# A second bias buffer, a finer spread of modulation parts and a new order of mixer steps in a two-layer diffusion backbone

## The chip, the cores and the metric

The kernel runs on one core of one Trainium2 chip. The metric is the device time of one execution in microseconds (us), taken as the median of the runs shown. TensorE does the matmuls (PE in the tables, its weight loads PEld), VectorE is DVE, ScalarE is ACT, GpSimd is POOL, and SyncE (SP) computes nothing: it issues the large loads. Each engine works through its own instructions in a fixed order and waits where an input is not there yet.

## The reference

One inference step through two layers, on 128 context tokens and 256 latent tokens of width 1024, in fp32. Of each layer:

```python
def trunk_layer(x, mods, mixer_w, g_norm_l, w_gu_l, w_down_l, ctx):
    sh1, sc1, ga1, sh2, sc2, ga2 = mods
    h = modulate(rms_norm(x, g_norm_l[0]), sh1, sc1)
    mix, new_ctx = token_mixers(h, *mixer_w, ctx)
    x = x + ga1 * rms_norm(mix, g_norm_l[1])
    f = swiglu(modulate(rms_norm(x, g_norm_l[2]), sh2, sc2), w_gu_l, w_down_l)
    x = x + ga2 * rms_norm(f, g_norm_l[3])
    return x, new_ctx
```

`token_mixers` projects `h` by one combined matrix and runs three head groups on it: neighbourhood attention with a learned relative bias (4 heads), grouped-query attention with normalised and rotated q and k (8 heads), and a bidirectional mLSTM scan (4 heads). The three outputs, concatenated, go through one output projection. `swiglu` has 2816 hidden columns. The six modulation vectors of a layer come from `silu(c) @ w_ada + b_ada`, once for the context and once for the latent tokens.

## The kernel before, in words

Every fp32 weight tile is split into a rounded part `hi` (ACT, line 117) and a remainder `lo` (DVE, line 118), and each product is three fp32r matmuls, `hi*hi`, `hi*lo`, `lo*hi` (`mm3`, lines 107 to 109). Weights arrive through SP in 512 KB pieces, in a ring of three `raw` tiles (`raw_of`, line 125). A piece can be issued when the split of the piece three before it is done.

A layer has two halves. **The mixers** (function `mixers`): projections, mLSTM, attention and output projection are cut into small steps, and the string `SCHEDULE[l]` lists these steps in the order in which they are recorded. PE, DVE and ACT execute in exactly that order (`ENGINES`, `manual_schedule`); the orders of SP and POOL are laid by the tile framework. The letters that matter here:

- `f` is the next piece of a projection (`fps` and `tps` tiles) or of the output projection (`ops`); of a projection by features one `f` is 6 matmuls of 384 columns. These pieces depend on little and fill PE.
- `t` is one tick of the modulation work (`Ada.tick`): load 1 MB of `w_ada` into one of two `araw` tiles, multiply the one before it on PE (`mul_p`, line 223, tile `adap` in the one PSUM bank of tag `sm`), add the result on DVE (`acc`, lines 229 and 231).
- `L0` to `L3` load row data for four mLSTM units into a `W` tile (POOL, line 867, then a select on POOL, line 870), `E` takes exponentials on ACT (line 887), `C` makes scores on PE (line 909, tile `S`) and multiplies them with `W` on DVE (lines 896, 897, 911), `U` sums on PE (lines 922 and 926, tile `nd`) and writes `hml` through DVE. `cin` transposes the incoming states on PE (line 948, tile `ctp`); `hsum`, `hrstd`, `hnorm` normalise `hml`, and the last reader of `hml` is line 1003 on DVE.
- `bias` loads the bias windows of the neighbourhood attention, one tile `nb` for each pair of heads (`load_bias`, four SP loads per tile at line 1090, each of 64 x 6 runs of 64 floats). `K0` and `K1` transpose the cached keys (line 687) and add the column mask to the bias (line 1094, DVE).
- `c`, `e`, `p`, `v` are scores, softmax, transposes and value products of an attention unit: `sc` (line 1021, PE), `nm` (line 1027, DVE), `P` (line 1035, ACT), `ptp` (line 1050), `av` (line 1063).
- `A1` to `A4` split weight pieces ahead, until so many pairs are ready.
- `r`, `g`, `x`, `q`, `y` finish a 128-token tile (norm, gate, residual, norm), and `00` to `11` transpose it (line 354), modulate it (`xm`, line 359, ACT) and split it into `hT` (lines 363 and 364, DVE) for the second half.

**The feed-forward half** (function `ffn`): 11 steps `b2`, each with the gate and up products of 256 hidden columns (`gups`, 384 tokens) and, two blocks late, the down products (`facc`). Here the modulation vectors are multiplied on DVE (`mul_v`, line 179) and summed on PE (line 188). Its first products (`gu`) need the `hT` of tiles 0 and 1, first the half of columns 0 to 511 and then the other.

The two bias tiles before: tile 0 is a buffer of pool `mp` with the tag "R", which holds the mLSTM's gate rows until `cols` has transposed them. Tile 1 is a buffer of pool `mn` with the tag "n3", which holds `hml`.

Of the kernel before, what the change touches and what calls it, by code (L numbers as in the profile page):

```python
# [8 lines left out]
F32 = mybir.dt.float32  # L9
# [8 lines left out]
DEPTH = 2  # L18
# [2 lines left out]
NEG = -1e30  # L21
SCHEDULE = (
    (
# [8 lines left out]
    ),  # L32
    (
# [8 lines left out]
    ),  # L42
)
ENGINES = {mybir.EngineType.PE, mybir.EngineType.DVE, mybir.EngineType.Activation}
# [7 lines left out]
def hybrid_step(  # L52
# [10 lines left out]
    cp = ctx.enter_context(tc.tile_pool(name="cp", bufs=1))  # L63
# [19 lines left out]
    brow = tp.tile([96, 128], F32, tag="g2", name="brow", bufs=4)  # L83
    A.dma_start(brow, b_ada.rearrange("l (e p) -> (l e) p", p=128))
    junk = cp.tile([128, D], BF16, name="junk")
    ones = cp.tile([128, 1], F32, name="ones")
    G.memset(ones, 1.0)
    eps = cp.tile([128, 1], F32, name="eps")
    G.memset(eps, EPS)
    scol = cp.tile([128, 8, 34], F32, name="scol")  # L90
    V.memset(scol, 0.0)
# [7 lines left out]
    Amod = cp.tile([128, 2, 2, 2, 8], F32, name="Amod")  # L99
# [167 lines left out]
    def ada_start(pp):  # L267

        big = [hp.tile([128, 3, 4, 256], F32, tag=f"hT{a}", name=f"sraw{a}") for a in range(2)]
        more = ov.tile([128, 4, 4, 256], F32, tag="ov", name="sraw2")  # L270
        slots = [b[:, n] for b in big for n in range(3)] + [more[:, n] for n in range(4)]
        b1 = cp.tile([128, 8], F32, name="b1")
        V.tensor_scalar(b1, bcol[:, 0, 1], 1.0, None, ALU.add)

        def load_q(q):
            r = {}
            for h in range(2):
                for vec in range(2):
                    n = 4 * q + 2 * h + vec
                    raw = slots[n % 10]  # L280
                    e0 = vec * D + q * 256
                    SP.dma_start(raw, w_ada[0, h * 512:(h + 1) * 512, e0:e0 + 256].rearrange("(k p) f -> p k f", p=128))
                    r[vec, h] = raw
            return r

        def mod_sum(raws, hs=(0, 1), ps=None):
            ps = ps or [pp.tile([128, 512], F32, tag="b", name="sps") for _ in range(2)]
            for h in hs:
                for vec in range(2):
                    for k2 in range(2):  # L290
                        for g in range(4):
                            k = 2 * k2 + g // 2
                            fs = slice((g % 2) * 128, (g % 2) * 128 + 128)
                            PE.matmul(ps[vec][32 * g:32 * g + 32, 0:128], lhsT=scol[:, 4 * h + k, 2:34],
                                      rhs=raws[vec, h][:, k, fs], start=h == 0 and k2 == 0, stop=h == 1 and k2 == 1)
            return ps

        def mod_cols(q, ps):
            cps = pp.tile([128, 512], F32, tag="b", name="scp")
            for vec in range(2):  # L300
                rows = ap_.tile([128, 128], F32, tag="acc", name="srows", bufs=2)
                A.activation(rows, ps[vec][:, 0:128], AF.Copy)
                PE.matmul(cps[:, 4 * vec:4 * vec + 4], lhsT=rows, rhs=cst[:, C_SC:C_SC + 4],
                          start=True, stop=True)
            for n in range(2):
                f = 2 * q + n
                b, a = (cps[:, 4 * vec + 2 * n:4 * vec + 2 * n + 2] for vec in range(2))
                V.tensor_scalar(Bmod[:, 0, 0, :, f], b, bcol[:, 0, 0, f:f + 1], None, ALU.add)
                am = V.tensor_scalar(Amod[:, 0, 0, :, f], a, b1[:, f:f + 1], gcol[:, 0, 0, f:f + 1],
                                     ALU.add, ALU.mult)  # L310
            return am.ins
        return load_q, mod_sum, mod_cols
# [60 lines left out]
    def mixers(l, ma, mp, mn, pp, banks, h1T, steps, pairs, tails):  # L373
        ada = Ada(steps, pp, "sm")
# [115 lines left out]
        def tok_first(c0):  # L490
            ps = [pp.tile([128, 512], F32, tag="w", name="tps") for _ in range(3)]
            if l == 0:
                load_q, mod_sum, mod_cols = ada_start(pp)
                ws = {}

# [586 lines left out]
        nbs = {}  # L1082

        def load_bias(j):
            nbs[j] = nb = (mn if j else mp).tile([128, 2, 6, 64], F32, tag="n3" if j else "R", name="nb")
            for u in range(2):
                for hd in range(2):
                    base = na_bias[l, 2 * j + hd]
                    src = bass.AP(base.tensor, base.offset + (5 - u) * 31 - 48, [[1, 64], [31, 6], [1, 64]])
                    SP.dma_start(nb[64 * u:64 * u + 64, hd], src)  # L1090
# [6 lines left out]
        for i in (1, 2):  # L1097
            for j in range(2):
                n_units.append(Unit([(lambda j=j, i=i: N["q"][:, j, tile_slice(i)], lambda j=j: N["k"][:, j, 128:512])], 3,
                                    lambda u, b, hd, j=j: vn[:, 1 + b, j * 128 + 64 * hd:j * 128 + 64 * hd + 64],  # L1100
# [13 lines left out]
        def load_biases():  # L1114
            for j in range(2):
                load_bias(j)
# [84 lines left out]
    def ffn(l, fa, fb, pp, steps, h2T, first, tail):  # L1201
# [3 lines left out]
        ada = Ada(steps, pp, "gu", spare)  # L1205
# [83 lines left out]
        def gu(b2, raws=None, ready=(), then=None):  # L1289
            raws = raws or gu_raw(b2)  # L1290
            ready = list(ready)
            for bb in range(2):
                pss = []
                for g in range(2):
                    w = ready.pop(0) if ready else gu_w(4 * b2 + 2 * bb + g, raws[g][:, :, bb * 128:(bb + 1) * 128])
                    ps = pp.tile([128, 512], F32, tag="gu", name="gups")
                    gmm(ps, w, 0, 384)
                    pss.append(ps)
                act(2 * b2 + bb, *(ps[:, :384] for ps in pss))
                if then and not bb:  # L1300
                    then()

        def down_w(b, dst=None):
            return load_k(w_down[l], b * 128, 1, 0, 1024, dst)

        def down_mm(b, w, i, halves=(0, 1)):
            hi, lo = w[:2]
            tk = slice(i * 128, (i + 1) * 128)
            f = fT[b]
            for half in halves:  # L1310
                mm3(facc[i][half], f[0][:, tk], f[1][:, tk], hi[:, 0, HALVES[half]], lo[:, 0, HALVES[half]],
                    b == 0, b == NB - 1)
# [3 lines left out]
        for b2 in range(1, NB // 2):  # L1316
            gu(b2, *(started if b2 == 1 else ()))
            if b2 < NB // 2 - 1:
                for b in (2 * b2 - 2, 2 * b2 - 1):
                    w = down_w(b)  # L1320
                    for i in range(3):
                        down_mm(b, w, i)
                        if b2 > 1 and i:
                            with tc.issue_after(w[2]), tc.issue_after(w[3]):
                                ada.tick(2 if l + 1 < DEPTH else 1)
        ada.finish()
        last = range(NB - 4, NB)
        flat = [[t.rearrange("p k f -> p (k f)") for t in slots[n]] for n in range(2)]
# [167 lines left out]
```

## Time and profile before

| | us |
|---|---|
| runs of the kernel before | 1021.54, 1014.47, 1019.5 |
| their median | 1019.5 |
| the profiled execution | 1013.69 |
| its span, first to last instruction | 1011.9 |
| mean granted TensorE clock, as a share of full speed | 0.981 |

The profile is of one execution, which lies 5.8 us under the median of the runs. In the profile a busy time is the sum over an engine's instructions, with overlaps counted once; "idle before" is the time in which an engine stood still ahead of an instruction, with what released it. The clock of TensorE has two levels, 1.2 and 2.4 GHz; the profile gives it as a share of the higher one, so that 0.50 is a stretch wholly at the lower level.

### The profile page before, as it was taken

To read this page: it belongs to the slowest core of one execution; us is meant where nothing else is said; L and a number is where in the kernel's file an instruction comes from. 1 tells how busy PE (TensorE), PEld (TensorE's weight loads), DVE (VectorE), ACT (ScalarE), POOL (GpSimd) and SP (SyncE) were. 2 spreads that over 40 slices of the span, in tenths; PEclk is the share of its full clock that TensorE was granted. 3 is DMA by queue.
4 is the path that set the end of the run, shared out by engine and by line. 5 is a ranking of instruction groups with operands and counts; after the bars stand their busy time and mean duration, and the time that the engine had idled before them with its cause. 6 is when DMAs were issued, how large, how long until landed. Compare 5 with 4: busy or idle time off the path is not lost. (4 is left out here: it accounts for less than half of the span.)

```text
span 1011.9 us, 16033 instructions
## 1 busy us (share of the span) xinstructions
PE 960.1 (95%) x6375; PEld 847.8 (84%) x6375; DVE 620.7 (61%) x940; ACT 466.3 (46%) x920; POOL 83.4 (8%) x142
## 2 busy tenths in 40 slices
PE   5999889899999999999999989899799999999997
PEld 4789776578999999999978979666699999999996
DVE  3568547667954999959374855677577433333323
ACT  4545426678533433333375553577573333333322
POOL 0312411000001100000320230000000001000000
PEclk9999999999999999999999997999899999999999
DMA  9969768407873976945235652330756335333001
GB/s 329 306 194 244 230 206 240 124 2 250 275 234 117 322 262 226 312 167 179 73 101 152 161 153 60 91 99 2 239 183 202 125 125 167 125 125 125 21 1 63
DMA packets 128508, 167.22 MB, mean 165 GB/s; under 512 B 15664, under 2 KB 90176, under 8 KB 128432
## 3 DMA queue, kind: packets, MB, share of 16 engines
q1 hardware_dynamic: 122208, 153.93, 47.9%
q0 software_dynamic: 5856, 12.10, 4.4%
q8 instruction: 50, 0.82, 0.3%
q14 instruction: 26, 0.21, 0.1%
q10 hardware_dynamic: 368, 0.16, 0.1%
HBM read 163.46 MB, written 2.70 MB: 164 GB/s over the span
## 5 line engine op out<-in xcount | busy, mean ns | idle before, releaser
L118 DVE TENSOR_TENSOR lo<-raw,hi 128x1024 fp32r<-128x1024 f32 (+2 forms) x100 | 120.1, 1204 | 80.1 <-ACT hi L117 79.8
L117 ACT ACTIVATE hi<-raw 128x1024 fp32r<-128x1024 f32 (+2 forms) x100 | 103.8, 1041 | 97.1 <-PE facc L109 80.3
L109 PE MATMUL gups<-hT,ring 128*128 128x384 f32 x416 | 140.8, 339 | 0.0
L107 PE MATMUL gups<-hT,ring 128*128 128x384 f32 x416 | 140.7, 338 | 0.0
L108 PE MATMUL gups<-hT,ring 128*128 128x384 f32 x416 | 140.6, 338 | 0.0
L179 DVE SCALAR_TENSOR_TENSOR spare<-araw,scol,spare 128x1024 f32<-128x1024 f32 x98 | 120.7, 1279 | 0.5 <-ACT spare L177 0.4
L107 PE MATMUL facc<-hi,f 128*128 128x512 f32 x240 | 95.6, 398 | 0.0
L108 PE MATMUL facc<-lo,f 128*128 128x512 f32 x240 | 94.8, 395 | 0.0
L109 PE MATMUL facc<-hi,f 128*128 128x512 f32 x240 | 94.8, 395 | 0.0
L108 PEld LDWEIGHTS gups<-hT,ring 128*128 128x128 f32 x416 | 78.2, 188 | 0.5
L107 PEld LDWEIGHTS gups<-hT,ring 128*128 128x128 f32 x416 | 78.1, 188 | 0.5
L109 PEld LDWEIGHTS gups<-hT,ring 128*128 128x128 f32 x416 | 78.2, 188 | 0.0
L109 PE MATMUL gups<-hT,xring 128*128 128x384 f32 x224 | 75.8, 338 | 0.0
L107 PE MATMUL gups<-hT,xring 128*128 128x384 f32 x224 | 75.8, 338 | 0.0
L108 PE MATMUL gups<-hT,xring 128*128 128x384 f32 x224 | 75.7, 338 | 0.0
L107 PE MATMUL tps<-hi,hT 128*128 128x512 f32 (+2 forms) x192 | 67.4, 351 | 2.2 <-DVE hT L511 2.2
L109 PE MATMUL tps<-hi,hT 128*128 128x512 f32 (+2 forms) x192 | 65.5, 341 | 0.0
L108 PE MATMUL tps<-lo,hT 128*128 128x512 f32 (+2 forms) x192 | 65.4, 340 | 0.0
L1228 ACT ACTIVATE ring<-rgu 128x1024 fp32r<-128x1024 f32 x26 | 27.6, 1062 | 68.2 <-PE gups L108 37.8
L1228 ACT ACTIVATE ring<-spare 128x1024 fp32r<-128x1024 f32 x26 | 27.6, 1060 | 62.3 <-PE gups L108 37.4
L107 PEld LDWEIGHTS facc<-hi,f 128*128 128x128 f32 x240 | 45.2, 188 | 10.8 <-issue 1.4
L109 PEld LDWEIGHTS facc<-hi,f 128*128 128x128 f32 x240 | 45.2, 188 | 10.5
(299 smaller groups left out, 1983.0 us busy)
## 6 DMA issues: line engine op xcount, KB each, us to landing
araw<-in_w_ada_dram SPq DMA_DIRECT2D x80, 512.0 KB, 4.9
raw<-in_w_down_dram SPq DMA_DIRECT2D x44, 512.0 KB, 4.2
spare<-in_w_gu_dram SPq DMA_DIRECT2D x20, 1024.0 KB, 5.4
rgu<-in_w_gu_dram SPq DMA_DIRECT2D x20, 1024.0 KB, 5.2
raw<-in_w_in_dram SPq DMA_DIRECT2D x36, 512.0 KB, 4.8
sraw<-in_w_ada_dram SPq DMA_DIRECT2D x16, 512.0 KB, 9.5
raw<-in_w_out_dram SPq DMA_DIRECT2D x8, 512.0 KB, 5.8
G<-row POOLq DMA_DIRECT2D x8, 512.0 KB, 7.2
```

The costliest lines, as they stand in the source:

```text
L107: PE.matmul(out, lhsT=wh, rhs=xh, start=start, stop=False)
L108: PE.matmul(out, lhsT=wh, rhs=xl, start=False, stop=False)
L109: PE.matmul(out, lhsT=wl, rhs=xh, start=False, stop=stop)
L117: a = A.activation(hi[:, :n], raw, AF.Copy)
L118: v = V.tensor_tensor(lo[:, :n], raw, hi[:, :n].bitcast(F32), ALU.subtract)
L179: V.scalar_tensor_tensor(acc[s], raw[:, part], scol[:, k, 2 + s:3 + s], acc[s], ALU.mult, ALU.add)
L1228: A.activation(hi, rv, AF.Copy)
```

## The change

Four edits. (1) Both bias tiles come from pool `mp`, tile 1 under a tag of its own, "nb", so it no longer shares a buffer with `hml`. (2) To make room, `ones` and `eps` become two columns of one tile, and the eight-column helper `b1` lies in a part of `Amod` that layer 1 writes later. (3) In the feed-forward half the ticks are dealt out differently: per weight block 1, 1, 2 after the three token tiles in place of 0, 2, 2 (layer 0), and 0, 0, 1 in place of 0, 1, 1 (layer 1). (4) Both strings of `SCHEDULE` are new: the same steps, each as often as before, in another order. The instructions of each engine are the same in number and kind; their order differs. Line numbers after the change are higher by one.

```diff
 SCHEDULE = (
     (
...
-        "L3 s s C1 s s U0 E2 C2 s s U1 s f t E3 t C3 U2 f f U3 s f s s f s s t s f f hsum kT s hrstd f s hnorm f "
-        "f bias t s f A1 A2 f K1 f A2 A2 f t rT K0 f rmix s f f A2 t c0 f e0 kout c1 A2 p0 t f f e1 v0 c2 p1 t "
...
+        "L3 s s s U0 E2 C2 s ogate U1 s f t E3 U2 C3 f s f s f f U3 f t s t f s hsum hrstd kT s hnorm f s f f t "
+        "bias f A2 s s A2 f A1 K1 A2 f K0 f rT t rmix f s f f s t c0 f A2 e0 A2 kout c1 p0 t f A1 f e1 v0 c2 A2 "
...
     (
...
-        "f s f Q1 s f f Q2 f f f krow f cols decay kw f cin E0 L1 f cout C0 L2 s ogate L3 s E1 f C1 s s E2 U0 s "
-        "s s s f C2 s E3 U1 s s s s U2 s f s C3 s s s f s kT f f U3 f f f s s f bias s hsum hrstd hnorm f f f f "
...
+        "f s Q0 f Q1 f Q2 f f f krow f cols decay kw L1 E0 cin f s f cout C0 E1 L2 s L3 f s C1 s ogate s s E2 s "
+        "s U0 s C2 f E3 U1 U2 s s s s s f s s C3 s f f s f kT f f s U3 hsum s s s hrstd hnorm bias f f f f f f f "
...
-    ones = cp.tile([128, 1], F32, name="ones")
+    ones_eps = cp.tile([128, 2], F32, name="ones_eps")
+    ones, eps = ones_eps[:, 0:1], ones_eps[:, 1:2]
     G.memset(ones, 1.0)
-    eps = cp.tile([128, 1], F32, name="eps")
...
-        b1 = cp.tile([128, 8], F32, name="b1")
+        b1 = Amod[:, 1, 0, 0]
...
-            nbs[j] = nb = (mn if j else mp).tile([128, 2, 6, 64], F32, tag="n3" if j else "R", name="nb")
+            nbs[j] = nb = mp.tile([128, 2, 6, 64], F32, tag="nb" if j else "R", name="nb")
...
-                        if b2 > 1 and i:
+                        if b2 > 1:
                             with tc.issue_after(w[2]), tc.issue_after(w[3]):
-                                ada.tick(2 if l + 1 < DEPTH else 1)
+                                ada.tick(1 + i // 2 if l + 1 < DEPTH else i // 2)
```

How the instructions stand, before and after, at three places.

SP in layer 0, around the bias loads, before the change (`nb_1607` is bias tile 0, `nb_1612` tile 1; `araw` are modulation weights):

```order
L125 DMA raw_1100<-in_w_in_dram 128x8x128
L168 DMA araw_1261<-in_w_ada_dram 128x2x512
L1090 DMA nb_1607<-in_na_bias_dram 64x6x64 x2
L125 DMA raw_1175<-in_w_in_dram 128x8x128
L125 DMA raw_1467<-in_w_out_dram 128x2x512
L168 DMA araw_1617<-in_w_ada_dram 128x2x512 x2
L125 DMA raw_1598<-in_w_out_dram 128x2x512
L1090 DMA nb_1612<-in_na_bias_dram 64x6x64 x4
L168 DMA araw_1669<-in_w_ada_dram 128x2x512 x2
L125 DMA raw_1771<-in_w_out_dram 128x2x512
```

And the same place after it (`nb_1631` is tile 1, `nb_1626` tile 0):

```order
L1091 DMA nb_1631<-in_na_bias_dram 64x6x64 x2
L126 DMA raw_770<-in_w_in_dram 128x8x128
L126 DMA raw_895<-in_w_in_dram 128x4x256
L169 DMA araw_1265<-in_w_ada_dram 128x2x512 x2
L1091 DMA nb_1626<-in_na_bias_dram 64x6x64 x3
L126 DMA raw_1173<-in_w_in_dram 128x8x128
L126 DMA raw_1446<-in_w_out_dram 128x2x512
L126 DMA raw_1596<-in_w_out_dram 128x2x512
L169 DMA araw_1605<-in_w_ada_dram 128x2x512 x2
L126 DMA raw_1769<-in_w_out_dram 128x2x512
```

Tile 1, which stood between the third and the fourth output weight, now stands ahead of the last nine pieces of the input weights; tile 0 keeps its place.

SP in layer 1, before (`nb_6096` is tile 0, `nb_6101` tile 1):

```order
L125 DMA raw_5787<-in_w_in_dram 128x8x128
L1090 DMA nb_6096<-in_na_bias_dram 64x6x64 x4
L125 DMA raw_6008<-in_w_out_dram 128x2x512
L125 DMA raw_6068<-in_w_out_dram 128x2x512
L125 DMA raw_6118<-in_w_out_dram 128x2x512
L1090 DMA nb_6101<-in_na_bias_dram 64x6x64 x4
L125 DMA raw_6203<-in_w_out_dram 128x2x512
```

And after (`nb_6094` is tile 1, `nb_6089` tile 0):

```order
L126 DMA raw_5072<-in_w_in_dram 128x3x256
L1091 DMA nb_6094<-in_na_bias_dram 64x6x64 x4
L126 DMA raw_5075<-in_w_in_dram 128x3x256
L126 DMA raw_5785<-in_w_in_dram 128x8x128
L1091 DMA nb_6089<-in_na_bias_dram 64x6x64 x4
L126 DMA raw_6006<-in_w_out_dram 128x2x512
L126 DMA raw_6116<-in_w_out_dram 128x2x512
```

Tile 1 moves to the first pieces of the layer's input weights, sixteen pieces ahead of where tile 0 stands.

ACT at the end of layer 0's mixers, before (`junk` are sums of squares, `ss` their roots, `hi` a weight split, `xm` the modulation that makes the second `hT` half of tile 1, the last `x8` those of tile 2):

```order
L117 ACTIVATE hi<-raw 128x1024
L327 ACTIVATE junk,ss<-oP 128x512 x2
L331 ACTIVATE ss<-ss 128x1
L332 ACTIVATE ss<-ss 128x1
L359 ACTIVATE xm<-trp,Bmod,Amod 128x128 x4
L327 ACTIVATE junk,ss<-x 128x512
L117 ACTIVATE hi<-raw 128x1024
L327 ACTIVATE junk,ss<-x 128x512
L359 ACTIVATE xm<-trp,Bmod,Amod 128x128 x8
```

And after:

```order
L328 ACTIVATE junk,ss<-oP 128x512 x2
L332 ACTIVATE ss<-ss 128x1
L333 ACTIVATE ss<-ss 128x1
L118 ACTIVATE hi<-raw 128x1024
L328 ACTIVATE junk,ss<-x 128x512
L118 ACTIVATE hi<-raw 128x1024
L360 ACTIVATE xm<-trp,Bmod,Amod 128x128 x4
L328 ACTIVATE junk,ss<-x 128x512
L360 ACTIVATE xm<-trp,Bmod,Amod 128x128 x8
```

Two splits and one sum of squares now stand between the root and the four `xm`.

## Rows read from the trace of the kernel before

**Rows 1.** The profile page: busy time of each engine.

```profile
PE 960.1 (95%) x6375; PEld 847.8 (84%) x6375; DVE 620.7 (61%) x940; ACT 466.3 (46%) x920; POOL 83.4 (8%) x142
```

**Rows 2.** Windows by stage: length, busy us (instructions), clock, DMA share, GB/s.

```profile
75.00:153.00 78.00, 68.44 (x704) 62.95 (x706) 46.91 (x100) 34.51 (x79) 22.57 (x34) 0.98 0.76 221
153.00:240.00 87.00, 81.58 (x734) 58.68 (x735) 62.17 (x121) 62.14 (x167) 3.48 (x5) 0.98 0.48 134
240.00:515.00 275.00, 274.68 (x1608) 253.84 (x1607) 207.15 (x222) 107.98 (x147) 19.78 (x35) 1.00 0.65 218
515.00:640.00 125.00, 118.63 (x749) 107.73 (x748) 77.53 (x148) 69.23 (x154) 20.71 (x31) 0.95 0.45 119
640.00:735.00 95.00, 82.71 (x621) 60.57 (x620) 64.63 (x122) 62.08 (x171) 0.76 (x1) 0.95 0.36 113
```

**Rows 3.** PE timeline: start us, us, instruction, [idle before <- releaser].

```profile
106.44 1.08 PE L223 MATMUL adap<-araw,scol 128*32 128x128 f32 x32 [1.09 <-DVE acc L231]
...
124.61 0.63 PE L926 MATMUL nd<-share,W 128*128 128x65 f32 x4 [2.35 <-DVE hml L937]
...
148.19 0.47 PE L687 MATMUL tT<-cst,kcn 128*128 128x128 f32 x1 [4.79 <-DVE acc L231]
...
182.14 1.56 PE L1021 MATMUL sc<-kTn,qTn 64*64 64x384 f32 x8 [3.56 <-ACT P L1035]
...
604.01 1.52 PE L909 MATMUL S<-qTm,kTm 64*64 64x128 f32 x32 [3.56 <-DVE W L896]
...
612.57 1.08 PE L926 MATMUL nd<-share,W 128*128 128x65 f32 x4 [1.90 <-ACT s L138]
...
624.57 0.42 PE L107 MATMUL fps<-hT,hi 128*128 128x384 f32 x1
...
626.56 0.33 PE L109 MATMUL fps<-hT,lo 128*128 128x384 f32 x1
...
644.89 1.10 PE L1021 MATMUL sc<-share 64*64 64x128 f32 x32 [3.98 <-ACT P L1035]
...
723.09 0.55 PE L107 MATMUL gu<-hT,hi 128*128 128x256 f32 x1 [5.38 <-DVE hT L363]
```

**Rows 4.** DVE timeline, layer 0 and layer 1.

```profile
135.03 0.96 DVE L1003 TENSOR_TENSOR share<-share,hml 128x768 f32<-128x768 f32 x1
...
144.61 0.56 DVE L1094 TENSOR_TENSOR nb<-nb,cst 128x384 f32<-128x384 f32 x1 [6.64 <-DMA nb<-in_na_bias_dram]
...
239.64 0.69 DVE L364 TENSOR_TENSOR hT<-xm,hT 128x512 fp32r<-128x512 f32 x1
...
642.62 0.68 DVE L1027 TENSOR_REDUCE nm<-sc 128x4 f32<-128x512 f32 x1
```

**Rows 5.** SP timeline, layer 0.

```profile
136.01 2.62 SPq L1090 DMA_DIRECT2D nb<-in_na_bias_dram  x4
```

**Rows 6.** Windows over four short stretches, columns as in rows 2.

```profile
148.00:153.00 5.00, 4.81 (x23) 4.56 (x27) 2.33 (x5) 0.98 (x2) 3.31 (x6) 0.70 0.69 260
...
155.00:180.00 25.00, 22.60 (x256) 15.57 (x254) 17.86 (x28) 14.78 (x45) 3.48 (x5) 1.00 1.01 266
...
605.00:610.00 5.00, 4.38 (x31) 4.01 (x23) 2.88 (x9) 2.51 (x10) 2.78 (x4) 0.50 0.60 134
...
645.00:650.00 5.00, 4.96 (x45) 3.97 (x46) 3.42 (x6) 2.80 (x14) 0.76 (x1) 0.66 0.81 224
```

**Rows 7.** ACT timeline, layer 0 and layer 1.

```profile
179.74 1.06 ACT L117 ACTIVATE hi<-raw 128x1024 fp32r<-128x1024 f32 x1 [4.34 <-DMA raw<-in_w_out_dram]
...
233.01 1.10 ACT L117 ACTIVATE hi<-raw 128x1024 fp32r<-128x1024 f32 x1
...
638.50 2.00 ACT L117 ACTIVATE wT<-raw 128x1024 fp32r<-128x1024 f32 x2
```

**Rows 8.** DMA issues: count, KB each, median us from issue to landing.

```profile
raw<-in_w_in_dram SPq DMA_DIRECT2D x36, 512.0 KB, 4.8
...
nb<-in_na_bias_dram SPq DMA_DIRECT2D x16, 96.0 KB, 5.8
```

25 rows, old and new, of the table SCHEDULE are left out of this document.

## The prediction

> **What bounds the kernel.** I read the busy times first, then a table of windows by stage, then the idle time in front of PE's instructions, and last the other engines' timelines at those places. PE is busy 960.1 of 1011.9 us [rows 1], so an order alone can win only what PE waits, some 52 us, and what it loses where a wait is followed by the lower clock. The stages [rows 2] show where that lies. In the feed-forward stretch 240 to 515 PE is busy 274.68 of 275 us: nothing can be won there. The mixers have it: 78 - 68.44 = 9.6 us idle in 75 to 153, 5.4 in 153 to 240, 6.4 in 515 to 640 and 12.3 in 640 to 735. All four have a clock under 1.00. The edits touch these stages, and [rows 3] names the single waits.
>
> Where PE is busy throughout, a stretch with mean clock c costs (1 - c) times its length, since that share of the time is at half speed for twice as long. I use this below for what a wait costs after it has ended.
>
> **The bias wait of layer 0: +6.3 us.** PE stands 4.79 us before a key transpose at 148.19, for `acc` on DVE [rows 3]. DVE had itself stood 6.64 us before the mask of a bias tile, for that tile's load [rows 4]. SP had issued the load at 136.01 [rows 5], just when line 1003, which began at 135.03 and took 0.96 us, had read `hml` for the last time [rows 4]: the shared buffer is the cause. With a tile of its own the load stands ahead of nine weight pieces, long before, and tile 0's loads keep their place. So the 4.79 us go. After the wait the clock of 148 to 153 is 0.70 [rows 6], with PE nearly always busy: 0.30 x 5 = 1.5 us more. Late next would be the cached keys, whose load PE's own transposes release; the projection pieces between these and the first use stay the same, so I expect no new wait. Bounds: 0, if another input is as late, to 6.3.
>
> **The bias wait of layer 1: +4.0 us.** PE stands 3.98 us at 644.89 for `P`, which needs `nm`, which DVE began at 642.62 [rows 3, 4] behind the same kind of mask. Without the bias, `P` is limited by the two splits on ACT that end at 638.50 + 2.00 = 640.50 [rows 7]. From the end of `nm` (642.62 + 0.68 = 643.30) to the PE start were 1.59 us, so PE could start at about 642.1, 2.8 us earlier. Some 1.1 us of wait is left. The window 645 to 650 has clock 0.66 [rows 6], a loss of 1.7; after so short a wait I expect it mostly back and take 1.2. Bounds 0 to 3.98 + 1.7 = 5.7.
>
> **The mLSTM of layer 0: +1.3 us.** The last sum waits 2.35 us at 124.61 [rows 3]. Two things help now: four `f` steps stand before it where two stood, and POOL reaches the fourth `W` load two small transfers earlier. Twelve projection matmuls start from 624.57 to 626.56 [rows 3], so two `f` are 1.99 x 12/11 = 2.2 us; the wait should vanish. Against that, two ticks later on now stand back to back. The pair that did so before made PE wait 1.09 us for the single bank of `adap` at 106.44 [rows 3]. Sum 2.35 - 1.09. Bounds -1.1 to 2.4.
>
> **The mLSTM of layer 1: +3.0 us.** PE waits 3.56 us for `S` at 604.01 and 1.90 at 612.57 [rows 3], and the clock of 605 to 610 is 0.50 [rows 6]. The chain starts at the state transposes, which release the second `W` buffer. One `f` step pair (12 matmuls of 256 columns; by the price above 2.2 x 256/384 = 1.4 us) moves from ahead of these transposes to behind the scores at 604. So the chain starts 1.4 us earlier, the wait at 604 stays about 3.56, and the piece fills time before 612.57: 1.4 us won. A shorter second wait should end the low clock sooner; of the 0.5 x 4.38 = 2.2 us that this window shows, and what follows it, I take 1.6. Against it: POOL now issues the third `W` load only behind the second one's select and a store. Bounds: -2 (that delay decides) to 3.56 + 1.90 + 2.2 = 7.7; I take a value near the 1.4 and the clock, which have rows.
>
> **The end of layer 0's mixers: -1.7 us.** `hT` of tile 1's second half was done at 239.64 + 0.69 = 240.33 [rows 4], and PE went into it without a wait, having nothing else. On ACT two splits now stand between the root and `xm`; one of them stood in ACT's time ahead of the sums before (233.01 [rows 7]), and a sum of squares comes along. One split is about 1.1 us there, the sum about 0.6: the half is later by 1.7, and PE has no cover. Bounds -2.7 (both splits) to 0.
>
> **No change.** The wait of 3.56 us at 182.14 [rows 3]: ACT stood 4.34 us for an output weight [rows 7], and SP still issues the same modulation loads ahead of it; bounds -4 to +4. The 5.38 us at 723.09 [rows 3]: the chain of splits, sums and modulation before it stands as it did. The finer ticks: PE has no idle time there to win [rows 2], and in layer 1 one tick for each weight block still suffices for four loads and eight products; -1 to +1. The merged constants and `b1`: start only, 0.
>
> **Sum.** 6.3 + 4.0 + 1.3 + 3.0 - 1.7 = 12.9 us. From the profiled execution, 1013.7 us, that gives 1000.8; it was 5.8 us under the median, and from the median 1019.5 it gives 1006.6. I state 1006.5.
>
> **Rivals.** *The loads take it back.* Once layer 0 runs 7.6 us ahead (6.3 + 1.3), the attention stage asks for its weights that much sooner, and 155 to 180 already has a DMA share of 1.01 [rows 6]. Then the wait at 182.14 grows by these 7.6 us, and 5.3 remain: 1014. For it: the share. Against it: the stretch before has 0.76 [rows 2], so loads could start sooner, as far as the two `araw` and three `raw` tiles allow.
>
> *The bias loads starve the projections (slower).* Tile 1 of layer 0 now goes into the queue ahead of nine weight pieces in a stretch that feeds them. One bias DMA of 96 KB lands in 5.8 us, one of 512 KB in 4.8 [rows 8]. A feature piece feeds 24 matmuls, 4.3 us by the price above; three `raw` tiles give a lead of two, 8.6 us. If each of five pieces behind the bias slipped by a landing, 29 us, less the lead, 20 us would fall on PE: 12.9 - 20 = -7, or 1027. It decides once the slip is over 8.6 us. Against it: four bias DMAs are together less than one piece in bytes, and the quad of tile 0 stands among the last input weights in both orders.
>
> The Trainium skill speaks for this rival: "DMA: Bandwidth & Descriptors", section Specifications, asks for at least 512 B in a run for line rate and says that below it the engine reads, modifies and writes. The runs here are 256 B. If that doubled the DMA time of the quad's 384 KB, it would be another 384 KB at the 221 GB/s of the first mixer stage, 1.8 us, and the sum by it, if PE felt all of it, 11.1. The rows agree with a dear small load (96 KB slower than 512 KB), but not that PE feels it.
>
> *The bias still comes late.* If the new tile lies on memory that the half before still uses, or SP reaches it late, both bias terms fall: 12.9 - 10.3 = 2.6, or 1017. The order of SP speaks against it.
>
> **How the numbers follow.** Forecast 0.60; loads take it back 0.26; starved projections 0.07; bias still late 0.07. The range is 996 to 1019: at the low end the forecast with the clock and both mLSTM terms near their upper bounds (a gain of 23), at the high end past the second and the fourth case. About 1% of 1019.5, 10.2 us, is what a measurement can tell from no change. The forecast by its bounds lies beyond that nine times in ten, 0.54, with a little of the second case 0.56; slower by over 1% is the larger half of the starved case, 0.04; within 1% the rest, 0.40.
>
> **What would show it.** Right: no DVE wait before line 1095 (the old 1094); no PE wait before the key transposes of layer 0; a wait of about 1 us before the group scores of layer 1; none before the fourth sum of layer 0; one of about 1.7 us in the `gu` matmuls of layer 0; the 5.4 us before `gu` of layer 1 unchanged. Wrong: a wait over 7 us for an output weight in layer 0 (the first rival), waits of ACT for input weights that reach PE before 100 us (the second), or a bias load issued behind line 1004 (the third).

## The result and the profile after

| | us |
|---|---|
| kernel before, median of 19 runs (1014.47 to 1022.97) | 1018.9 |
| kernel after, median of 19 runs (1005.7 to 1014.45) | 1009.56 |
| ratio after / before, 95% interval | 0.9912 [0.9895, 0.9929] |
| first profiled execution, before / after | 1013.69 / 1013.52 |
| second profiled execution, before / after | 1017.87 / 1008.12 |

The change saves 9.0 us (0.0088 of 1018.9). I had said 12.9 us: 1006.5, in a range of 996 to 1019. The time lies in the range, 3 us above the point. The interval excludes no change; the saving of 0.9% falls just inside the "within 1%" that had 0.40, not in the "faster" that had 0.56, and the interval holds the border between the two.

The first two profiled executions hide all of this: they differ by 0.2 us, since that of before lies 5.2 us under its kernel's median and that of after 4.0 us over its own. I therefore read the change from the second pair, whose difference of 9.7 us is close to the 9.3 of the medians, and go back to more profiles below where a reading rests on it. The stages are cut at the same places of the work: first `sc` of layer 0, first `gu`, first `gups` from the extra ring, first transpose of layer 1, its first `sc`, its first `gu`, the end. Columns as in [rows 2]. The kernel before, second execution:

```profile
0.00:154.60 154.60, 132.88 (x1267) 116.21 (x1267) 83.64 (x184) 69.94 (x148) 34.71 (x64) 0.98 0.82 247
154.60:235.00 80.40, 75.14 (x660) 52.46 (x656) 56.54 (x112) 56.59 (x153) 3.48 (x5) 0.98 0.44 121
235.00:253.10 18.10, 18.10 (x130) 16.99 (x129) 13.39 (x22) 14.54 (x33) 0.00 (x0) 1.00 0.94 315
253.10:518.30 265.20, 264.89 (x1538) 244.48 (x1537) 201.42 (x215) 100.08 (x134) 19.77 (x35) 1.00 0.64 212
518.30:641.10 122.80, 114.29 (x717) 104.35 (x715) 75.83 (x144) 65.14 (x144) 20.70 (x31) 0.94 0.45 120
641.10:727.20 86.10, 73.42 (x560) 51.06 (x559) 62.08 (x119) 61.53 (x167) 0.76 (x1) 0.95 0.29 81
727.20:1016.10 288.90, 282.67 (x1518) 263.14 (x1518) 127.99 (x148) 98.30 (x145) 3.79 (x6) 0.98 0.38 123
```

And the kernel after, second execution:

```profile
0.00:149.80 149.80, 131.27 (x1263) 114.95 (x1263) 85.10 (x184) 69.71 (x148) 35.31 (x64) 0.98 0.83 255
149.80:231.30 81.50, 76.73 (x660) 53.72 (x656) 57.10 (x112) 55.75 (x152) 3.48 (x6) 0.96 0.45 120
231.30:251.70 20.40, 18.44 (x131) 17.08 (x130) 13.62 (x24) 15.52 (x34) 0.00 (x0) 1.00 0.84 281
251.70:516.90 265.20, 264.89 (x1538) 244.49 (x1537) 201.19 (x215) 100.34 (x134) 19.77 (x35) 1.00 0.65 213
516.90:636.40 119.50, 112.36 (x718) 102.62 (x717) 76.21 (x146) 65.16 (x144) 21.15 (x31) 0.96 0.47 126
636.40:716.90 80.50, 70.76 (x560) 48.99 (x559) 61.19 (x117) 61.17 (x167) 0.76 (x1) 1.00 0.26 77
716.90:1006.40 289.50, 283.24 (x1518) 263.71 (x1518) 128.68 (x148) 98.14 (x145) 3.79 (x6) 0.98 0.38 123
```

Length minus PE's busy time is what PE waited. Where the number of instructions is equal, I take a change of PE's busy time for the clock's. So every stage splits in two, the first only roughly, since its counts differ by four. Up to the first `sc` of layer 0, 4.8 us are won: 21.7 us of waits became 18.5. The attention stage of layer 0 loses 1.1 in this pair, by the clock (one low stretch of 6.8 us in place of one of 3.4). The entry of the feed-forward half loses 2.3, of which 2.0 are a new wait. The long feed-forward stage is the same to the hundredth. The mixers of layer 1 win 3.3 and then 5.6, the latter with 2.9 us fewer waits and 2.7 us less busy time for the same 560 instructions. Over the whole span, 6.0 us of the 9.7 are waits and 3.7 the clock.

PE's waits in the kernel after, second execution (columns as in [rows 3], which have those of before):

```profile
107.85 1.08 PE L224 MATMUL adap<-araw,scol 128*32 128x128 f32 x32 [0.56 <-DVE acc L232]
...
118.50 0.30 PE L242 MATMUL adat<-cst,acc 128*128 128x128 f32 x1 [1.12 <-DVE ht L941]
...
131.15 1.08 PE L224 MATMUL adap<-araw,scol 128*32 128x128 f32 x32 [0.80 <-DVE acc L232]
141.32 0.30 PE L688 MATMUL tT<-cst,kcn 128*128 128x128 f32 x1 [0.97 <-DMA kcn<-in_cache_na_kv_dram]
...
238.88 0.38 PE L108 MATMUL gu<-hT,hi 128*128 128x256 f32 x1 [1.62 <-DVE hT L364]
...
602.65 2.41 PE L910 MATMUL S<-qTm,kTm 64*64 64x128 f32 x32 [4.07 <-DVE W L897]
608.38 0.63 PE L927 MATMUL nd<-share,W 128*128 128x65 f32 x4 [0.82 <-DVE hml L938]
612.27 0.63 PE L927 MATMUL nd<-share,W 128*128 128x65 f32 x4 [1.48 <-DVE ht L941]
...
640.33 1.10 PE L1022 MATMUL sc<-share 64*64 64x128 f32 x32 [1.03 <-ACT P L1036]
...
716.93 0.55 PE L108 MATMUL gu<-hT,hi 128*128 128x256 f32 x1 [5.39 <-DVE hT L364]
```

The two waits of the bias are gone: 4.79 us in [rows 3] are now 0.97, for the cached keys and no longer for the bias, and 3.98 are 1.03. The wait of 1.62 us at `gu` of layer 0 is new, and the 5.39 at `gu` of layer 1 stand as they did. On DVE the mask of the bias, which waited 6.64 us in [rows 4], now runs without a wait:

```profile
138.85 1.96 DVE L1095 TENSOR_TENSOR nb<-nb,cst 128x384 f32<-128x384 f32 x4
```

### The profile page after: what moved, and what is told of

It reads as the page before. It is cut to its first block, busy times and chain, and to the rows that moved or that the text cites. A ratio compares the mean times of both kernels' runs of the same rounds, so it can differ in the third digit from the quotient of the medians.

```text
span 1011.7 us, 16033 instructions
## 1 busy us (share of the span) xinstructions
PE 961.7 (95%) x6375; PEld 849.1 (84%) x6375; DVE 623.4 (62%) x940; ACT 466.0 (46%) x920; POOL 83.5 (8%) x142
## 5 line engine op out<-in xcount | busy, mean ns | idle before, releaser
L118 ACT ACTIVATE hi<-raw 128x1024 fp32r<-128x1024 f32 (+2 forms) x100 | 103.8, 1042 | 100.4 <-PE facc L110 85.1
L1244 DVE TENSOR_TENSOR sg<-sg,gups 128x384 f32<-128x384 f32 x40 | 22.1, 553 | 54.1 <-PE gups L110 54.0
L108 PEld LDWEIGHTS facc<-hi,f 128*128 128x128 f32 x240 | 45.1, 188 | 10.6 <-issue 1.2
```

What stands on the lines that cost most here:

```text
L108: PE.matmul(out, lhsT=wh, rhs=xh, start=start, stop=False)
L118: a = A.activation(hi[:, :n], raw, AF.Copy)
L1244: V.tensor_tensor(sg, sg, pu, ALU.mult)
```

## The experiments

Ratios are to the kernel before, run beside each on the same chip, with 95% intervals.

### How far one profile is from its median

Both kernels unchanged, executed and profiled once more.

> The kernel before once more, for a second profile. If what a profile lies off its median by is the low clock, the low stretches of this one total more than the 40.3 us of the first profile when its time is above 1013.7 us. If not, the total is the same and the difference is in the waits.

> The kernel after once more, for a second profile. The first one, 1013.5 us, lies 4 us above its median, with a low clock at 119.5 and 6.8 us of it at 180.9. If low stretches are what the time moves by, this one, near 1009.6 us, has 5 to 8 us less of low clock than the first; if not, the total is the same.

Before: 1017.87 us. After: 1008.12 us. The low stretches in the clock record total 43.6 us (40.3 in the first profile) and 36.2 us (41.0), so both moved the way the times did, that of after by slightly less than the 5 to 8 expected. But the clock is only a part. Before, PE's busy time rose from 960.1 [rows 1] to 961.4, by 1.3 of the 4.2 us that the span grew, and the rest are waits. After, it fell from 961.7 to 957.7, 4.0 of 5.3 us. One pair of profiles can't show a change of 1%.

### The buffer alone

Both strings and the ticks are those of before; the merged constants that make room are in.

```diff
-            nbs[j] = nb = (mn if j else mp).tile([128, 2, 6, 64], F32, tag="n3" if j else "R", name="nb")
+            nbs[j] = nb = mp.tile([128, 2, 6, 64], F32, tag="nb" if j else "R", name="nb")
```

> The kernel before with the second bias buffer alone (and the merged constants that make room for it); both old orders of steps and the old ticks. My theory: the two bias waits go, 4.8 us plus clock in layer 0 and about 2.8 us plus clock in layer 1, together 10.3 us, so a ratio near 0.990 to before; in the profile no DVE wait before the mask line and no PE wait of 4.8 us before the key transposes of layer 0. Rival, the loads take it back: the wait for the output weight in layer 0 (3.56 us before) grows by most of what is won, ratio 0.995 to 0.998. Rival, the new order and not the buffer brings the gain: within 0.2% of before.

1006.61 us, ratio 0.9882 [0.9853, 0.9911]: 12 us, with an interval of 3 us on either side, so as much as the whole change saves, or more. In its profile PE has no wait of 0.3 us or more between the fourth mLSTM sum and the first `sc` of layer 0, and 1.03 us before the group scores of layer 1. The wait for the output weight in layer 0 is 4.33 us against 3.4 to 4.0 in three profiles with the shared buffer, and two later profiles with a buffer of its own and the old order of layer 0 have 2.22 and 3.31: the loads take back less than 1 us, if anything. Both rivals fall.

### The ticks alone

```diff
-                        if b2 > 1 and i:
+                        if b2 > 1:
...
-                                ada.tick(2 if l + 1 < DEPTH else 1)
+                                ada.tick(1 + i // 2 if l + 1 < DEPTH else i // 2)
```

> The kernel before with the finer spread of ticks in the feed-forward half alone. My theory: no change, -1 to +1 us, ratio 0.999 to 1.001, since PE has no idle time in that stretch. Rival: the ticks now fall on other token tiles and delay the splits of the down weights or the last modulation vectors, so that the end of the half is 1 to 3 us later, ratio 1.001 to 1.003.

1017.62 us, ratio 0.9993 [0.9966, 1.0020]. Nothing that can be measured, as expected. The interval alone would leave room for most of the 1 to 3 us of the rival, but the profile does not: its two feed-forward stages take 265.3 and 288.9 us, against 265.2 and 288.9 above.

### The old order in one layer at a time

The kernel after with one of the two strings of `SCHEDULE` taken from before, of layer 0:

> The kernel after with the old order of steps in layer 0 alone. By my terms the new order of layer 0 is worth +1.3 (fourth sum of the mLSTM) and -1.7 us (end of the mixers), so this is within 1 us of the kernel after: ratio to before near 0.990. Rival, the new order of layer 0 costs more than that: it brings a wait of about 1.6 us in the first gu matmuls, waits of 1.4 us before the modulation sums and a low clock behind them; then this kernel is 3 to 5 us faster than the kernel after, ratio to before 0.986 to 0.988. Rival, the new order of layer 0 is where the gain comes from: ratio 0.995 or more.

and of layer 1:

> The kernel after with the old order of steps in layer 1 alone. By my terms the new order of layer 1 is worth 3.0 us in the mLSTM, so this is 3 us slower than the kernel after: ratio to before near 0.994. Rival, the later load of the third row tile on the POOL queue eats it: no difference to the kernel after, ratio 0.991.

With the old layer 0: 1004.36 us, ratio 0.9863 [0.9829, 0.9897], 5 us faster than the kernel after, with an interval of some 4 us on that difference. The new order of layer 0 costs, as the first rival said. With the old layer 1: 1009.79 us, ratio 0.9915 [0.9882, 0.9947], beside 0.9912: no difference that these intervals can show.

### The new orders with the shared buffer

```diff
-            nbs[j] = nb = mp.tile([128, 2, 6, 64], F32, tag="nb" if j else "R", name="nb")
+            nbs[j] = nb = (mn if j else mp).tile([128, 2, 6, 64], F32, tag="n3" if j else "R", name="nb")
```

> The kernel after with the bias tiles sharing a buffer with hml again, as before (both new orders and the new ticks stay). My theory: the buffer is the gain, so both bias waits come back, 4.8 us before the key transposes less 2 us for the f steps that the new order puts between them and hnorm, and about 4 us in layer 1: 7 to 10 us slower than the kernel after, ratio to before 0.998 to 1.002. Rival, the new order already hides the bias load: within 2 us of the kernel after, ratio 0.991 to 0.993.

1017.82 us, ratio 0.9995 [0.9973, 1.0017]: without the buffer nothing is left of the gain. But the place isn't the one I expected in layer 0. PE's waits there, and before the group scores of layer 1:

```profile
141.84 0.30 PE L688 MATMUL tT<-cst,kcn 128*128 128x128 f32 x1 [1.25 <-DMA kcn<-in_cache_na_kv_dram]
...
173.96 0.88 PE L1064 MATMUL av<-PT,vn 128*64 128x128 f32 x12 [1.49 <-ACT PT L1054]
181.08 1.56 PE L1022 MATMUL sc<-kTn,qTn 64*64 64x384 f32 x8 [4.04 <-ACT P L1036]
...
649.24 0.99 PE L1022 MATMUL sc<-share 64*64 64x128 f32 x28 [3.43 <-ACT P L1036]
```

Before the key transposes there are 1.25 us, little more than the 0.97 with the buffer, so the new order does hide the bias load in layer 0. Longer waits stand 30 us later, 1.49 and 4.04 us. SP's timeline shows what is late there:

```profile
132.53 1.14 SPq L169 DMA_DIRECT2D araw<-in_w_ada_dram  x2
136.88 3.37 SPq L1091 DMA_DIRECT2D nb<-in_na_bias_dram  x4
140.35 6.62 SPq L169 DMA_DIRECT2D araw<-in_w_ada_dram  x4
147.08 0.41 SPq L126 DMA_DIRECT2D raw<-in_w_out_dram  x1
```

The same stretch in the kernel after:

```profile
132.29 7.61 SPq L169 DMA_DIRECT2D araw<-in_w_ada_dram  x4
140.00 0.42 SPq L126 DMA_DIRECT2D raw<-in_w_out_dram  x1
```

and of the kernel with the shared buffer, the row for this load in the view of waits of SP's queue (us in total, times, longest):

```profile
SPq L1091 <- DVE share L1004: 3.2, 1, 3.2
```

SP stands 3.2 us at the bias load until line 1004 has read `hml`, and takes another 3.4 for the four issues. The framework has also laid the output weight behind one more pair of modulation weights. It goes at 147.08 in place of 140.00, 7 us later.

These waits are not the shared buffer's alone, though. The first profile of the kernel after, where no bias load stands in this stretch, has nearly the same at this place, once for modulation weights and once for an output weight:

```profile
171.48 0.86 PE L224 MATMUL adap<-araw,scol 128*32 128x128 f32 x24 [1.33 <-DMA araw<-in_w_ada_dram]
...
182.43 1.56 PE L1022 MATMUL sc<-kTn,qTn 64*64 64x384 f32 x8 [3.87 <-ACT P L1036]
```

One profile therefore can't tell what the hold of SP costs.

### The bias load on another queue

The kernel of the last experiment, its bias still in the shared buffer, with tile 1's loads issued by POOL:

```diff
-                    SP.dma_start(nb[64 * u:64 * u + 64, hd], src)
+                    (G if j else SP).dma_start(nb[64 * u:64 * u + 64, hd], src)
```

> The kernel with the shared buffer and both new orders (ratio 0.9995), but tile 1's bias loads issued by POOL instead of SP. The load is as late as with SP, it only no longer stands in SP's queue. If the lateness of the bias itself is what the shared buffer costs: no change, ratio 0.998 to 1.001. If SP's queue, held at this load until hml has been read (136.9 us in layer 0) with weights behind it, is a good part of the cost: the waits of PE at 172 to 181 us (1.49 and 4.04 us) fall to about 2.8 us together, 2 to 3 us less, ratio 0.996 to 0.9975.

1014.43 us, ratio 0.9963 [0.9942, 0.9985]: about 3 us less, as the queue theory expected. SP's output weight is out at 139.35 again, ahead of the second pair, and PE's rows are

```profile
140.42 0.30 PE L688 MATMUL tT<-cst,kcn 128*128 128x128 f32 x1 [1.07 <-DMA kcn<-in_cache_na_kv_dram]
...
176.92 0.88 PE L1022 MATMUL sc<-kTn,qTn 64*64 64x384 f32 x8 [2.67 <-ACT P L1036]
...
644.71 1.10 PE L1022 MATMUL sc<-share 64*64 64x128 f32 x32 [4.13 <-ACT P L1036]
```

The waits of layer 0 are those of the kernel after in its second profile (0.97 us above, and 2.75 here); that of layer 1 stays.

```profile
177.45 1.56 PE L1022 MATMUL sc<-kTn,qTn 64*64 64x384 f32 x8 [2.75 <-ACT P L1036]
```

By the medians, then, the shared buffer costs the new orders some 3 us through SP's queue (0.9995 to 0.9963) and some 5 us otherwise (0.9963 to 0.9912). The 5 us lie in layer 1: from its first `sc` to its `gu` the two kernels with the shared buffer take 83.9 and 84.5 us, the kernel after 80.6 and 80.5. The 3 us are less sure. The two intervals overlap, and up to `gu` of layer 0 the two kernels take 234.7 and 229.6 us, where the two profiles of the kernel after have 235.8 and 231.3. And since SP's order changed along with the load's queue, the hold of SP and the extra pair of modulation weights are not told apart.

### Step 11 of layer 0 back ahead of the splits

One step of the kernel after moved:

```diff
-        "p13 A1 q1b b2 y1 10 A1 v13 A2 01 b2 b2 r2a r2b g2a x2a g2b x2b A1 A3 A2 A1 A1 q2a A4 11 q2b A3 A1 y2 A2 "
+        "p13 A1 q1b b2 y1 10 A1 v13 A2 01 b2 b2 r2a r2b g2a x2a g2b x2b 11 A1 A3 A2 A1 A1 q2a A4 q2b A3 A1 y2 A2 "
```

> The kernel after with one step of layer 0 moved: 11, which makes the second half of tile 1's hT, stands ahead of the weight splits again as it did before the change. My theory: the wait of 1.61 us before gu in layer 0 goes, with the low clock that follows it in some executions up to 3.4 us: ratio to the kernel after 0.9965 to 0.9985, to before 0.988 to 0.990. Rival, the splits that now come later are what the start of the feed-forward half waits for: no gain, ratio to before 0.991.

1006.3 us, ratio 0.9887 [0.9849, 0.9925], 2.5 us better than 0.9912, within the expected 0.988 to 0.990, though its interval holds 0.9912 too. The profile agrees: more than half of the new loss in the stage is gone (19.1 us from `gu` to the ring, against 20.4 in the kernel after and 18.1 before): the first `gu` products no longer wait, and a short wait for a weight split is left:

```profile
234.94 0.39 PE L110 MATMUL gu<-hT,lo 128*128 128x256 f32 x1 [0.75 <-DVE lo L119]
```

### The wait of 5.4 us in layer 1

The wait stood in both kernels, and my prediction put it down to a chain that has to be there. ACT's timeline of the kernel after shows something else:

```profile
711.65 0.64 ACT L328 ACTIVATE junk<-oP 128x512 bf16<-128x512 f32 x1
...
713.65 0.63 ACT L328 ACTIVATE junk<-oP 128x512 bf16<-128x512 f32 x1 [1.27 <-DVE ss L330]
...
714.40 0.30 ACT L332 ACTIVATE ss<-ss 128x1 f32<-128x1 f32 x1
714.73 0.20 ACT L333 ACTIVATE ss<-ss 128x1 f32<-128x1 f32 x1
714.84 1.49 ACT L360 ACTIVATE xm<-trp,Bmod,Amod 128x128 f32<-128x128 f32 x4
```

PE had made the transposes for this `xm` (step `01`, tile 1, the half that `gu` needs first) at 710.95, but ACT does them only after the sums of squares of tile 2, which wait for the last output products. The Trainium skill calls ACT, DVE and GpSimd "strict FIFO" ("Perfetto Trace Analysis", section "Tensor Engine Instruction (MATMUL, LD_WEIGHTS)"), and the trace agrees: `xm` was ready for over 3 us and stood in line. So I exchanged the two steps `01` and `11`:

```diff
-        "p11 f g1b x1b e12 x1a 00 f c13 q1a v11 p12 e13 A1 b2 v12 A1 10 p13 q1b b2 y1 v13 A2 b2 A1 A3 11 b2 r2a "
-        "g2a r2b g2b x2a x2b 01 q2a q2b y2 A4 A1"
+        "p11 f g1b x1b e12 x1a 00 f c13 q1a v11 p12 e13 A1 b2 v12 A1 10 p13 q1b b2 y1 v13 A2 b2 A1 A3 01 b2 r2a "
+        "g2a r2b g2b x2a x2b 11 q2a q2b y2 A4 A1"
```

With the old order of layer 0:

> The kernel after with the old order in layer 0 (ratio 0.986) and, in layer 1, the steps 01 and 11 exchanged: the first half of tile 1's hT, which gu needs first, is made ahead of tile 2's sums, the second half behind them. Theory: the 5.4 us before gu of layer 1 are not the chain of tile 1 but ACT's order, in which xm stands behind tile 2's two sums of squares; the wait falls to about 1 us, and with it the 6.8 us of low clock that follows: 4 to 7 us, ratio 0.980 to 0.982. Rival: the second half or tile 2 is what the end waits for, and the wait only moves some 6 us on, into gu: no gain, ratio 0.985 to 0.987.

and with the new one, `11` of layer 0 first:

> The same exchange of 01 and 11 in layer 1, with the new order of layer 0 in which 11 stands ahead of the weight splits (ratio 0.989). Theory as for the run before it: 4 to 7 us less, ratio 0.982 to 0.985; beside that run it tells whether the rest of layer 0's new order costs anything: equal within 0.2% if only the place of 11 did, 2 us slower if the modulation waits of the new order cost too. Rival: no gain, 0.988 to 0.990.

999.57 us, ratio 0.9815 [0.9788, 0.9841], and 996.98 us, ratio 0.9795 [0.9771, 0.9819], the fastest of all kernels run. Against the same kernels without the exchange (0.9863 and 0.9887) that is 4.9 and 9.4 us less, where 4 to 7 were expected, each with an interval of some 4.5 us on either side. In the profiles the two last stages together became 6.4 and 7.0 us shorter, which fits the forecast and both medians. In the profile of the second the wait and the low clock behind it are gone; its two last stages, cut as above:

```profile
631.20:707.40 76.20, 70.90 (x560) 48.98 (x560) 56.80 (x109) 58.05 (x157) 0.76 (x1) 1.00 0.23 61
707.40:994.40 287.00, 280.65 (x1518) 261.20 (x1518) 132.99 (x156) 101.38 (x155) 3.79 (x6) 0.99 0.40 130
```

```profile
707.41 0.35 PE L108 MATMUL gu<-hT,hi 128*128 128x256 f32 x1 [0.83 <-DVE hT L364]
```

The stage that ends at `gu` is 4.3 us shorter than in the kernel after (80.50), and the stage behind it takes 2.6 us less of PE for the same 1518 instructions. Nothing waits later in their place: 6.3 to 6.4 us idle in the last stage in both.

The two kernels also say what the rest of layer 0's new order is worth: 0.9815 with the old, 0.9795 with the new and `11` first; without the exchange it was 0.9863 against 0.9887, the other way round. Beyond the place of `11` these runs tell no difference between the two orders of layer 0.

### The order of layer 1 once more

> The fastest kernel so far (ratio 0.9795, 11 first in layer 0, 01 and 11 exchanged in layer 1) with the old order of layer 1, in which 01 and 11 are exchanged too. It measures the new order of layer 1 by itself once more. By my term of 3.0 us for the mLSTM of layer 1 this kernel is 3 us slower, ratio 0.982 to 0.983. Rival: the row tile's load and the exponentials behind it set the pace, and filling in behind the scores only moves the wait: the same within 1 us, ratio 0.979 to 0.981.

999.66 us, ratio 0.9824 [0.9785, 0.9862], 2.9 us above 0.9795, as my term has it, but the rival lies in the interval too. Together with the pair 0.9915 and 0.9912 (0.3 us) and the pair 0.9882 and 0.9863 (1.9 us, with the ticks in it), that is 1.7 us on average, each with an interval of some 3 to 4 us. The stage from layer 1's first transpose to its first `sc` shows no gain: with a bias buffer of its own, three profiles with the old order have 119.5 to 120.2 us and six with the new one 118.0 to 122.1, with a mean of 119.9 for both. The stage behind it, up to `gu`, is 0.7 us shorter with the new order, with and without the exchange (81.3 and 81.4 against 80.5 to 80.8; 76.8 against 76.0 and 76.2). The medians leave it open between 0 and 3 us; the profiles show 0.7.

## Why the prediction was right, and where it was not

- **Layer 0's bias wait, +6.3.** The wait went as I had said: 3.8 us in the second pair, and with it the low clock behind it (0.70 in [rows 6]; 1.00 from 141 to 146 now). With the 1.6 us less that PE is busy up to the first `sc` (four matmul records fewer), that makes 5.4. What I named as late next, the cached keys, is late now, by 0.97 us; I had priced it at nothing. And the buffer is not the only thing that does it: with the new order the wait is gone in the shared buffer too (1.25 us left), which I had not seen.
- **Layer 1's bias wait, +4.0.** Of the right size. From its first `sc` to `gu` the kernels with the old order take 85.1, 86.1 and 85.5 us with the shared buffer and 81.3 and 81.4 with one of its own: 4.2 us, with the 1.03 of wait left that I had forecast as 1.1. The 5.6 us of the second pair hold in addition the new order's 0.7 and a stretch of low clock that was 3.4 us longer in that execution of before. The two buffer terms together were 10.3; the buffer alone measured 12.0, with 10.3 inside its interval.
- **Layer 0's mLSTM, +1.3.** It is 0. The wait of 2.35 us did vanish. But I set one pair of ticks against it, and in the new order there are more waits in its place: 0.56 and 0.80 us for `acc`, 1.12 for the `ht` of the mLSTM that stands ahead of it on DVE, and two of 0.69 for a copy on ACT (line 691). Between 85 and 140 us the waits of PE over 0.2 us sum to 4.8 us before and 4.9 after, both in the second profile. The stage up to the first `sc`, which holds this term and the first, won 4.2 us in the mean (three profiles of the old order with the shared buffer, 154.5; six with both changed, 150.3), where the two terms make 7.6.
- **Layer 1's mLSTM, +3.0.** With the one before it, this is the term that I had most too large: 0.3, 1.9 and 2.9 us in three comparisons of medians, 0.7 in the profiles. The step that failed is "the wait at 604 stays about 3.56, and the piece fills time before 612.57". The chain is POOL's load of the row tile, its select, ACT's exponentials and a product on DVE:

```profile
590.03 1.44 POOL L868 DMA_DIRECT2D W<-mrow  x2 [11.49 <-PE ctp L949]
...
598.16 0.86 POOL L871 TENSOR_SCALAR_AFFINE_SELECT W<-W 128x768 f32<-128x768 f32 x1 [4.17 <-DMA W<-mrow]
```

```profile
599.05 2.07 ACT L888 ACTIVATE W<-W,share 128x128 f32<-128x128 f32 x6 [4.90 <-POOL W L871]
```

  From the load's issue at 590.03 to PE's scores at 602.65 are 12.6 us, and PE fills that time with projection pieces; a piece that is moved behind the scores, as I read it, leaves so much more of it empty. With a bias buffer of its own the wait before the scores is 4.02 us in the mean of six profiles with the new order and 2.43 in three with the old (with the shared buffer 5.35 in two and 3.91 in three): 1.6 us, all that the piece was to fill later. (Why the buffer alone shortens this wait too, no run shows; it was not in my sum, and may be part of what the buffer measured above 10.3.) Over the whole stage up to the first `sc` PE waits 7.2 us with the new order and 5.5 with the old. What did come is the clock, for which I had taken 1.6: for practically the same number of matmuls PE is busy 112.7 us in place of 114.4. In the mean the one cancels the other. One profile of each, first the old order and then the new:

```profile
516.30:636.30 120.00, 114.41 (x721) 104.72 (x719) 76.57 (x146) 65.24 (x144) 20.80 (x31) 0.94 0.46 126
```

```profile
512.00:631.20 119.20, 112.75 (x721) 102.76 (x719) 76.43 (x146) 65.25 (x144) 20.69 (x31) 0.96 0.46 126
```

- **The end of layer 0's mixers, -1.7.** The wait came where and as long as I had said (1.62 us). The loss is 2.3 us in the stage (18.1 to 20.4), a little more than I had said, and 2.5 by the medians when the step is moved back.
- **No change.** The 5.39 us before `gu` of layer 1 stayed, and the ticks are worth nothing. The wait for the output weight in layer 0 is 2.75 us in the second profile, with a longer low clock behind it, and 3.87 in the first, with another 1.33 ahead of it, in place of 3.56 and 3.37 before. The attention stage takes 81.5 and 83.6 us there, and 78.2 to 81.0 in four other profiles with the new order of layer 0 and a bias buffer of its own, against 80.4 in both of before: no change that profiles can show.
- **Rivals.** The loads take less than 1 us back, if anything. Of starved projections there is a trace, one wait of ACT of 2.73 us behind the bias loads that SP issues at 56.64:

```profile
56.64 1.70 SPq L1091 DMA_DIRECT2D nb<-in_na_bias_dram  x2
```

```profile
66.93 1.06 ACT L118 ACTIVATE hi<-raw 128x1024 fp32r<-128x1024 f32 x1 [2.73 <-DMA raw<-in_w_in_dram]
```

  It is under the lead of 8.6 us, and PE didn't wait. The bias is not late.

So the buffer is the gain, with 12.0 us where I had 10.3. The orders were to add 2.6 (1.3, 3.0 and -1.7), and by the ratios they take 3 us away, with an interval of some 3.5 us on either side: -2.5 to -5.0 for layer 0, for which I had -0.4, and some +1.7 for layer 1. My 12.9 came out too large because I counted what a new order removes, wait by wait, and too little of what it puts in. That the time lies only 3 us off is in part luck: I had 1.7 too little for the buffer and 5.6 too much for the orders, and the two errors go against each other.

## What to carry to other kernels

A buffer that is shared with something read late can cost twice: the load's reader waits (some 4 us here in layer 1), and what stands behind the load on the issuing queue goes late (an output weight by 7 us here, which by the medians may have cost some 3 us); look at what the queue holds back, not only at the wait with the buffer's name. Before a wait is put down to a chain of work, look at what stood ahead of the late instruction on its own in-order engine: exchanging two steps was worth 5 to 9 us here, where the whole change was worth 9. For effects of 1%, compare medians, and use single profiles only to say where, with PE's busy time at equal instruction counts as the measure of the clock.

## What the runs showed that I had not expected

A wait costs more than its length, and not always the same. In the second pair the stage before `gu` of layer 1 had 2.9 us fewer waits after the change and 2.7 us less busy time for the same 560 matmuls, at a clock of 1.00 in place of 0.95 (in the first pair 2.7 and 1.8, at 0.98 in place of 0.97); the exchange that took away 4.6 us of wait gave another 2.6 us behind it, at 0.99 in place of 0.98. And the same kernel differs from execution to execution: with the same instructions, PE was busy 961.7 and 957.7 us in two executions of the kernel after.
